# Loads on SyncE's queue, stores on ScalarE's: a change of issuing engines in a softmax with relative position bias

## The chip, the core and the metric

The kernel runs on one core of one Trainium2 chip. The metric is the device time of one execution in microseconds (us). VectorE, ScalarE and GpSimd compute here; SyncE only issues transfers; sixteen DMA engines move the bytes. TensorE does nothing.

## The reference

```python
B, H, S = 2, 8, 2112                       # logits: (B, H, S, S), float32
rel = clip(pos[:, None] - pos[None, :], -16, 16) + 16
x = logits + rel_bias[:, rel][None]        # rel_bias: (H, 33)
e = exp(x - x.max(-1, keepdims=True))
out = e / e.sum(-1, keepdims=True)         # float32
```

It reads 285.5 MB and writes 285.5 MB, and does little with each element.

## The kernel before

Each of the 128 partitions owns 264 rows. A chunk is six of them (6.49 MB over all partitions), so there are 44 chunks, and four buffers, `L0` to `L3`, go round. For a chunk, VectorE adds the bias (two adds of three rows), ScalarE takes the exps of the six rows with their sums, VectorE inverts the sums and scales; then the chunk is stored from the buffer it was loaded into. The maximum is not subtracted. A strip `F` of biases is built once at the start from the small table.

What the change touches is who issues the transfers:

```python
def store(eng, u, start, parts=1):
    take(eng, scaled, 1)                   # VectorE has scaled the chunk
    k = R // parts
    for r in range(0, R, k):
        eng.dma_start(out=rows(out, start + r, k * S), in_=L[u][:, r*S:(r+k)*S]).then_inc(stored[u], 16)

def reload(eng, u, start):
    take(eng, stored[u], 16)               # the buffer's last store has landed
    load(eng, u, start)

def sync_part(eng):
    row_load(eng, 0, first)                # rows 0, 2, 4 of chunk 0
    eng.wait_ge(loaded[BUFS - 2], 16)      # "the gate": the third load has landed
    passes(eng, 0, lambda u, start, loads: store(eng, u, start), N - BUFS)
    # ... (cut: the last four stores, and the waits for them)

def gpsimd_part(eng):
    row_load(eng, 1, loaded[0])            # rows 1, 3, 5 of chunk 0
    # ... (cut: two iotas for the strip)
    for n in range(1, BUFS):
        if n == BUFS - 1:
            take(eng, made, 1)             # buffer 3 was scratch for the strip
        load(eng, n, n * R)
    passes(eng, BUFS, lambda u, start, loads: reload(eng, u, start))
    eng.drain()

def scalar_part(eng):
    table_load(eng, range(B))
    # ... (cut: one small exp, which loads the activation table)
    passes(eng, 0, lambda u, start, loads: exps(eng, u))
```

## Time and profile before

| kernel before | |
|---|---|
| time, median of 3 runs | 1325.94 us (1325.87 to 1328.24) |
| bytes moved | 570.99 MB |
| VectorE, ScalarE, GpSimd busy | 71%, 40%, 3% |
| DMA queues' share of the engines | 50.4% + 49.3% |

First the list of DMA issues: what is moved, the issuing engine, how many, the size of each, and the median time in us from issue to landing.

```profile
L<-in_logits_dram POOLq DMA_DIRECT2D x43, 6336.0 KB, 39.1
out_dram<-L SPq DMA_DIRECT2D x42, 6336.0 KB, 55.3
```

A transfer of 6.49 MB would take 15 us with all engines to itself. It takes 39 or 55, because it queues behind others: in the steady state a transfer is nearly always waiting before the engines are free. Then the start, from the timeline (start us, length us, instruction, and in brackets the idle time before it and what ended that):

```profile
17.23 0.26 DVE L179 TENSOR_SCALAR L<-L,rbP 128x71 f32<-128x71 f32 x1 [12.51 <-DVEq L88]
...
24.88 13.43 DVE L118 TENSOR_TENSOR L<-L,F 128x6336 f32<-128x6336 f32 x2 [0.81 <-DVEq L88]
```

VectorE waits until 17.23 us for the bias table, finishes the strip and begins the first chunk's add at 24.88.

### The profile page before, as it was taken

The page shows a single profiled execution, that of the slowest core. Times are in us where ns is not written, and L with a number is a line of the kernel's source. Part 1 is how long each engine was busy: PE and PEld are TensorE (multiplying, and loading weights), DVE is VectorE, ACT ScalarE, POOL GpSimd, SP SyncE. Part 2 cuts the span into 40 slices and gives each one's busy share as a digit, 9 for nine tenths or more (in the row PEclk, how much of TensorE's full clock was granted, in tenths as well). Part 3 has the DMA queues.
Part 4 walks back from the last instruction along what each step waited for, and adds up shares of the span by engine and source line. Part 5 has one row for each costly group of instructions (what it writes and reads, how often), then busy time and mean ns, then how long its engine had stood idle before and what let it go on. Part 6 is the DMA issues. An engine that isn't in the chain of part 4 may idle for free. (4 is left out here: it accounts for less than half of the span.)

```text
span 1325.7 us, 2004 instructions
## 1 busy us (share of the span) xinstructions
DVE 941.8 (71%) x451; ACT 524.9 (40%) x530; POOL 35.1 (3%) x50
## 2 busy tenths in 40 slices
DVE  4989776677777767667777767667777767666891
ACT  0645533333444433333344443333344443333360
POOL 0000000000000000000000000000000000000000
DMA  9999999999999999999999999999999999999998
GB/s 392 434 432 430 439 433 433 433 437 431 428 439 439 431 427 439 437 431 430 439 434 427 437 439 430 428 439 437 433 428 437 437 430 433 437 433 428 432 444 349
DMA packets 13762, 570.99 MB, mean 431 GB/s; under 512 B 1600, under 2 KB 1600, under 8 KB 1600
## 3 DMA queue, kind: packets, MB, share of 16 engines
q1 hardware_dynamic: 7024, 288.72, 50.4%
q0 software_dynamic: 6592, 282.23, 49.3%
q10 hardware_dynamic: 144, 0.02, 0.0%
q14 instruction: 2, 0.02, 0.0%
HBM read 285.49 MB, written 285.47 MB: 431 GB/s over the span
## 5 line engine op out<-in xcount | busy, mean ns | idle before, releaser
L125 ACT ACTIVATE L<-L 128x2112 f32<-128x2112 f32 x264 | 515.2, 1952 | 767.9 <-ACTq L88 767.9
L118 DVE TENSOR_TENSOR L<-L,F 128x6336 f32<-128x6336 f32 x88 | 590.8, 6755 | 231.2 <-DMA L<-in_logits_dram 230.4
L139 DVE TENSOR_SCALAR L<-L,tot 128x2112 f32<-128x2112 f32 x264 | 332.7, 1317 | 13.2 <-DVEq L88 0.8
L135 DVE RECIPROCAL tot<-tot 128x3 f32<-128x3 f32 x88 | 15.2, 173 | 96.9 <-DVEq L88 96.9
L91 POOL DMA_DIRECT2D L<-in_logits_dram x43 | 33.8, 786 | 1208.2 <-POOLq L88 1208.2
L125 ACT ACTIVATION_READ_ACCUMULATOR L<-L 128x1 f32 x264 | 49.2, 186 | 0.0
L179 DVE TENSOR_SCALAR L<-L,rbP 128x71 f32<-128x71 f32 x1 | 0.3, 259 | 12.5 <-DVEq L88 12.5
L187 DVE TENSOR_TENSOR F<-L,rbP 128x2343 f32<-128x2343 f32 x1 | 2.6, 2601 | 0.1
L188 DVE TENSOR_TENSOR F<-F,L 128x2343 f32<-128x2343 f32 x1 | 2.6, 2600 | 0.1
L252 ACT ACT_TABLE_LOAD x1 | 1.3, 1283 | 2.9 <-issue 2.9
L174 DVE TENSOR_SCALAR L<-L 128x71 int32<-128x71 int32 x1 | 0.2, 197 | 3.1 <-DVEq L88 3.1
L177 DVE TENSOR_SCALAR L<-L 128x71 f32<-128x71 f32 x3 | 0.6, 198 | 0.4
L208 POOL DMA_DIRECT2D L<-in_logits_dram x1 | 0.9, 880 | 1.1 <-PEq L291 1.1
L182 DVE SCALAR_TENSOR_TENSOR L<-L,rbP 128x71 f32<-128x71 f32 x1 | 0.3, 294 | 0.2 <-DVEq L88 0.2
L175 DVE TENSOR_TENSOR L<-L 128x71 f32<-128x71 int32 x1 | 0.2, 236 | 0.1
L180 DVE COPY F<-rbP 128x16 f32<-128x16 f32 x1 | 0.2, 175 | 0.1
L186 DVE COPY F<-rbP 128x16 f32<-128x16 f32 x1 | 0.2, 176 | 0.1
L234 POOL IOTA L<- 128x71 int32 x1 | 0.2, 207 | 0.1
L237 POOL IOTA L<- 128x71 int32 x1 | 0.2, 208 | 0.0
L252 ACT ACTIVATE one<-const-float32-0.0 128x1 f32<-128x1 f32 x1 | 0.2, 203 | 0.0
L280 POOL MEMSET const-float32-0.0<- 128x1 f32 x1 | 0.1, 98 | 0.4 <-issue 0.4
L280 POOL MEMSET const-bfloat16-1.0<- 128x1 bf16 x1 | 0.1, 101 | 0.0
(2 smaller groups left out, 0.2 us busy)
## 6 DMA issues: line engine op xcount, KB each, us to landing
L<-in_logits_dram POOLq DMA_DIRECT2D x43, 6336.0 KB, 39.1
out_dram<-L SPq DMA_DIRECT2D x42, 6336.0 KB, 55.3
out_dram<-L SPq DMA_DIRECT2D x4, 3168.0 KB, 46.4
L<-in_logits_dram SPq DMA_DIRECT2D x1, 3168.0 KB, 15.7
L<-in_logits_dram POOLq DMA_DIRECT2D x1, 3168.0 KB, 18.3
rbP<-in_rel_bias_dram ACTq DMA_DIRECT2D x2, 8.2 KB
```

What stands on the lines that cost most here:

```text
L91: eng.dma_start(out=L[u][:], in_=rows(logits, start)).then_inc(loaded[u], 16)
L118: eng.tensor_tensor(out=x3, in0=x3, in1=F3, op=ALU.add).then_inc(added, 1)
L125: e = eng.activation(out=x, in_=x, func=EXP, accum_out=tot[u][:, i : i + 1])
L135: eng.reciprocal(out=t, in_=t).then_inc(inverted, 1)
L139: e = eng.tensor_scalar_mul(out=x, in0=x, scalar1=tot[u][:, i : i + 1])
L177: step(eng.tensor_scalar(out=m, in0=qm, scalar1=0.0, scalar2=None, op0=op))
L179: step(eng.tensor_scalar(out=rest, in0=lt, scalar1=low, scalar2=None, op0=ALU.mult))
L182: eng.scalar_tensor_tensor(out=rest, in0=gt, scalar=high, in1=rest, op0=ALU.mult, op1=ALU.add)
L187: step(eng.tensor_tensor(out=blocks, in0=wide(eq), in1=rev, op=ALU.mult))
L188: step(eng.tensor_tensor(out=blocks, in0=blocks, in1=wide(rest), op=ALU.add))
L208: eng.dma_start(out=bass.AP(tensor=x.tensor, offset=x.offset + r0 * S, ap=[[list(x.ap[0])[0], P], [2 * S, R // 2], [1, S]],), in_=bass.AP( ...
L252: eng.activation(out=one, in_=nc.const_aps.tensor(0.0, [P, 1], FP32), func=EXP)
```

## The change

The intent is to have loads and stores on the two hardware queues, one each, and to leave GpSimd's queue, whose descriptors are made in software, unused. SyncE issues all loads, the first chunk as two transfers of alternate rows. ScalarE issues each store after the exps of the chunk, once VectorE has scaled it.

```diff
     def sync_part(eng):
         row_load(eng, 0, first)
-        eng.wait_ge(loaded[BUFS - 2], 16)
-        passes(eng, 0, lambda u, start, loads: store(eng, u, start), N - BUFS)
-        ... (cut: the last four stores)
-    def gpsimd_part(eng):
         row_load(eng, 1, loaded[0])
-        ... (cut: the iotas, which stay with GpSimd)
         for n in range(1, BUFS):
             if n == BUFS - 1:
                 take(eng, made, 1)
             load(eng, n, n * R)
         passes(eng, BUFS, lambda u, start, loads: reload(eng, u, start))
-        eng.drain()
+        ... (cut: the waits for the last four stores)
     def scalar_part(eng):
-        passes(eng, 0, lambda u, start, loads: exps(eng, u))
+        def whole(u, start, loads):
+            exps(eng, u)
+            if u == 0:
+                eng.wait_ge(loaded[BUFS - 2], 16)
+            store(eng, u, start)
+        passes(eng, 0, whole, N - BUFS)
+        for n in range(BUFS):
+            exps(eng, n)
+            store(eng, n, (N - BUFS + n) * R, 2 if n < 2 else 1)
```

More of the change, by code (lines that the diff above doesn't have):

```diff
@@ L222, in sync_part @@
         row_load(eng, 0, first)
-        eng.wait_ge(loaded[BUFS - 2], 16)
-        passes(eng, 0, lambda u, start, loads: store(eng, u, start), N - BUFS)
-        for n in range(BUFS):
-            store(eng, n, (N - BUFS + n) * R, 2 if n < 2 else 1)
+        row_load(eng, 1, loaded[0])
+        for n in range(1, BUFS):
+            if n == BUFS - 1:
+                take(eng, made, 1)
+            load(eng, n, n * R)
+        passes(eng, BUFS, lambda u, start, loads: reload(eng, u, start))
         for n in range(BUFS):
@@ L232, in gpsimd_part @@
     def gpsimd_part(eng):
-        row_load(eng, 1, loaded[0])
         eng.iota(qi, pattern=[[0, NB]], base=0, channel_multiplier=M).then_inc(
@@ L239, in gpsimd_part @@
         )
-        for n in range(1, BUFS):
-            if n == BUFS - 1:
-                take(eng, made, 1)
-            load(eng, n, n * R)
-        passes(eng, BUFS, lambda u, start, loads: reload(eng, u, start))
-        eng.drain()
     def scalar_part(eng):
```

## The prediction

> **What bounds the kernel now.** I read the page of the profile first: busy shares, the forty slices, then the queues.
>
> ```profile
> DVE 941.8 (71%) x451; ACT 524.9 (40%) x530; POOL 35.1 (3%) x50
> ...
> DMA  9999999999999999999999999999999999999998
> GB/s 392 434 432 430 439 433 433 433 437 431 428 439 439 431 427 439 437 431 430 439 434 427 437 439 430 428 439 437 433 428 437 437 430 433 437 433 428 432 444 349
> ...
> q1 hardware_dynamic: 7024, 288.72, 50.4%
> q0 software_dynamic: 6592, 282.23, 49.3%
> q10 hardware_dynamic: 144, 0.02, 0.0%
> ```
>
> No compute engine is near full, while the DMA row is 9 in every slice but the last, and the two large queues together fill 99.7% of the sixteen engines' time. 570.99 MB have to move; the rate lies about 434 GB/s in 38 slices, 392 in the first, 349 in the last. Next I cut the run into stretches, to see the rate without the ends and with one queue alone (columns: stretch, its length, busy us of VectorE, ScalarE and GpSimd, the clock, DMA share, GB/s).
>
> ```profile
> 20.00:50.00 30.00, 26.54 (x13) 11.90 (x12) 0.53 (x1) 1.00 1.00 433
> 100.00:1240.00 1140.00, 818.17 (x385) 459.36 (x463) 31.12 (x38) 1.00 1.00 434
> 1275.00:1320.00 45.00, 22.53 (x12) 11.90 (x12) 0.00 (x0) 1.00 1.00 432
> ```
>
> The middle line is the steady state, loads from GpSimd's queue and stores from SyncE's side by side: 434 GB/s. The first is loads alone (the DMA view of that stretch lists only the software queue), the third stores alone from SyncE's hardware queue. All three give the same rate with the engines full, so the sixteen DMA engines are the bound, whatever the mix of queues. 570.99 MB / 434 GB/s = 1315.6 us; the other 10 us are ends: in the first 3.3 us the engines are little used (the DMA view from 0 to 33 us starts with digits 0 0 7 5), 8,448-byte packets run at some 410 GB/s from 5 to 15 us, and after 1320 us only 17 GB/s flow, the last landing.
>
> How far is compute from being the bound? The list of waits and one chunk of the timeline (start, length, engine, instruction):
>
> ```profile
> POOL L L91 <- POOLq L88: 1208.2, 41, 56.5
> ACT L L125 <- ACTq L88: 767.9, 88, 27.3
> DVE L L118 <- DMA L<-in_logits_dram: 230.4, 38, 6.4
> ...
> 505.65 13.43 DVE L118 TENSOR_TENSOR L<-L,F 128x6336 f32<-128x6336 f32 x2 [6.23 <-DMA L<-in_logits_dram]
> ...
> 525.62 3.78 DVE L139 TENSOR_SCALAR L<-L,tot 128x2112 f32<-128x2112 f32 x3 [0.15 <-DVEq L88]
> ```
>
> From the first add to the last scaling of a chunk are 525.62 + 3.78 - 505.65 = 23.75 us; a chunk comes every 30 us (two loads and stores of 6.49 MB at 434 GB/s: 29.9). VectorE waits 6.2 us per chunk for the load: that is the slack of the compute chain. The load's median from issue to landing is 39.1 us, the store's 55.3; over 30 us that is 1.3 loads and 1.8 stores in flight on average, so both queues hold work nearly always.
>
> **What the Trainium skill says.** (1) "DMA: Bandwidth & Descriptors", section "Issuing engines are not separate DMA queues": transfers from ScalarE, SyncE and GpSimd run on the same sixteen engines and interleave; spreading the issue saves only sequencer time. The three stretches agree: 433, 434, 432. (2) Same page, "Where 436 GB/s comes from": sixteen ports give 435.2 GB/s. The 434 agrees, and it leaves at most 0.3% (1315.6 - 570.99/435.2 = 3.6 us) for any better queue. The same section says the HBM side, about 358, binds such transfers; this trace, one core alone, does not show that. (3) "SBUF — State Buffer", section "SBUF: two separate sides": while VectorE runs an instruction in a two-port mode, GpSimd can't write its descriptors; a hardware queue isn't affected. The trace agrees: a load issue lasts 0.53 us usually, yet the one at 825.41 took 1.35 and ended at 826.76, just after the first of the scalings that began at 825.32 (1.315 us each, so 826.64). (4) First page, "Latency and other measured facts": first byte after some 0.6 us on a hardware queue, some 1 us on GpSimd's.
>
> **The change, part by part.**
> - Loads: 43 issues leave GpSimd (786 ns mean, 33.8 us busy in all) for SyncE, where an issue took 332 ns. On average a load starts 786 - 332 = 0.45 us sooner, 1 us where the scaling blocked it. Nothing of it is on the path that sets the end: when a load is issued the one before has 39.1 - 30 = 9 us to go, and stores are queued. Value: 0.
> - Stores: 46 issues go to ScalarE, behind each chunk's exps. Cost on ScalarE: 332 ns as on SyncE, up to 0.91 us as its own two table loads took (median), so 15 to 42 us over the run on an engine busy 525 of 1326 us. ScalarE also stands still until the chunk is scaled. But VectorE runs in order: the next chunk's first add (6.75 us) begins only after that scaling, and the exps need that add. So at least 6.75 - 0.91 = 5.8 us are left over for the issue in every chunk. Value: 0.
> - First chunk: both halves stand in SyncE's queue one behind the other. The bytes are the same and sixteen engines work from the first half on; it lands by about 2 + 3.24 MB / 410 GB/s = 10 us instead of 16.8, the second by about 18 instead of 19.9. The bias table's packets (18 on each engine that carries them: 144 over 8, the 8 my reading of the access pattern) now alternate with one large queue, not two: estimate 9 to 12 us instead of 17.2. The strip of biases takes 17.23 to 24.08, 6.9 us, so the first add should start at 18 to 20 us instead of 24.88. This is not turned into time: the first store still waits for the third load, at about 50 us, and the DMA engines are full from 3.3 us. I give 0 to -1 us.
> - Gate on the first store now holds ScalarE: the exps of chunk 1 could begin about 49 us and begin at about 50.5; before they began at 55.4. No loss.
> - End: same four last stores, same halves; loads end some 45 us before the end. GpSimd's drain goes, beside nothing. Value: 0.
>
> Sum: 1325.9 + 0 + 0 - 0.5 + 0 is about 1325; with noise of the runs (1325.87 to 1328.24) I keep 1325.
>
> **Rivals.**
> (a) The software queue had a hidden cost, and two hardware queues come nearer to the ceiling: at most 3.6 us for the rate and 1 us at the start: 1321. For it: blocked issues. Against: engines at share 1.00 with it.
> (b) ScalarE becomes part of the chain: if the issue cost or blocked for longer than the 5.8 us left and the 6.2 us slack, say 15 us per chunk, a chunk would take 23.75 + 15 - 5.8 = 33 us, or 1450 in all. For it: an issue could be held up while descriptors are made or a ring is full. Against: SyncE issued the same stores in 332 ns (482 at most), also with four of them queued at the end.
> (c) Two hardware queues disturb each other, one share starving the other or reads and writes mixing worse. If stores were favoured, loads would land later; once they take more than 6 us longer the slack is gone only if in-flight work runs out, since four buffers hold 120 us: 39.1 + 55.3 + 23.75 = 118. A loss of 1% in rate makes 1338. Against: nothing in this trace shows two large hardware queues together, so I can't exclude it; this is my main doubt.
> (d) Earlier compute at the start shortens the whole: would be up to 6 us if compute were the bound; the full DMA row speaks against it.
>
> **Range and chances.** 1325 us, eight times in ten between 1320 (all of rival a) and 1332 (half a percent for rival c). Faster by over 2% would need 1299, below the 1311.9 us which the bytes take at 435.2: 0.01. Slower by over 2%, above 1352, needs (b) or a strong (c): 0.04. Within 2%: 0.95.
>
> **What would show it.** Right: DMA share 1.00 and 433 to 435 GB/s from 100 to 1240 us; the queues' shares 50/50, now both hardware; load plus store landing still about 94 us; VectorE still waiting about 6 us per chunk for loads; GpSimd's 34 busy us gone; store issues on ScalarE under 1 us; the first add at 18 to 20 us, the first store still near 50. Wrong: a steady rate under 430, slices below 9 in the middle, ScalarE's issue over 2 us, or VectorE's waits moved from loads to sums.

## The result, and the profile after

The changed kernel took 1327.14 us (median of 4 runs, 1326.46 to 1328.04), the kernel before 1327.09 us in 4 runs (1325.87 to 1329.13). The ratio is 0.9999, with a 95% interval from 0.9982 to 1.0017: the same. Ratios here are the mean time of one kernel's fast runs over the mean of the other's fast runs of the same rounds, so not quite the ratio of the medians that are quoted.

The page of the changed kernel, the same lines as in the prediction:

```profile
DVE 941.5 (71%) x451; ACT 524.9 (40%) x530; POOL 0.5 (0%) x6
...
DMA  9999999999999999999999999999999999999998
GB/s 395 433 430 432 436 438 424 436 441 436 424 438 439 427 435 438 436 424 438 441 425 433 439 436 424 438 439 435 425 439 438 425 435 439 438 424 436 433 434 363
...
q1 hardware_dynamic: 6992, 285.48, 49.9%
q10 hardware_dynamic: 6768, 285.49, 49.8%
```

GpSimd's 35 us are gone, both large queues are hardware now, and the DMA rows look as before. The stretches (loads alone, steady state, stores alone) say it in numbers; the last column is GB/s:

```profile
20.00:50.00 30.00, 26.84 (x11) 11.90 (x12) 0.00 (x0) 1.00 1.00 433
...
100.00:1240.00 1140.00, 815.75 (x385) 459.99 (x465) 0.00 (x0) 1.00 1.00 434
...
1275.00:1320.00 45.00, 20.96 (x10) 11.90 (x12) 0.00 (x0) 1.00 1.00 433
```

They were 433, 434 and 432. The waits, one chunk of the timeline, and the DMA issues:

```profile
DVE L L117 <- DMA L<-in_logits_dram: 234.3, 39, 6.3
```

```profile
503.89 13.43 DVE L117 TENSOR_TENSOR L<-L,F 128x6336 f32<-128x6336 f32 x2 [6.23 <-DMA L<-in_logits_dram]
...
523.86 3.78 DVE L138 TENSOR_SCALAR L<-L,tot 128x2112 f32<-128x2112 f32 x3
...
527.88 0.34 ACTq L96 DMA_DIRECT2D out_dram<-L  x1
533.86 13.43 DVE L117 TENSOR_TENSOR L<-L,F 128x6336 f32<-128x6336 f32 x2 [6.22 <-DMA L<-in_logits_dram]
540.73 1.96 ACT L124 ACTIVATE L<-L 128x2112 f32<-128x2112 f32 x1 [17.34 <-ACTq L87]
```

```profile
L<-in_logits_dram SPq DMA_DIRECT2D x43, 6336.0 KB, 37.2
out_dram<-L ACTq DMA_DIRECT2D x42, 6336.0 KB, 58.0
```

The add of one chunk begins 29.97 us after that of the one before, and VectorE still waits 6.2 us for the load in each. ScalarE issues the store at 527.88, in 0.34 us, and its next exp begins only at 540.73, when the next add is done: 12.5 us lie between. Loads land 1.9 us sooner, stores 2.7 us later; the sum, 95.2 us, is nearly the 94.4 of before.

The start did move:

```profile
13.01 0.26 DVE L178 TENSOR_SCALAR L<-L,rbP 128x71 f32<-128x71 f32 x1 [9.87 <-DVEq L87]
...
20.66 13.43 DVE L117 TENSOR_TENSOR L<-L,F 128x6336 f32<-128x6336 f32 x2 [0.81 <-DMA L<-in_logits_dram]
...
44.32 13.42 DVE L117 TENSOR_TENSOR L<-L,F 128x6336 f32<-128x6336 f32 x2
50.44 0.38 ACTq L96 DMA_DIRECT2D out_dram<-L  x1
51.20 1.96 ACT L124 ACTIVATE L<-L 128x2112 f32<-128x2112 f32 x1 [11.04 <-ACTq L87]
```

The table came 4.2 us sooner, the first add too; now it waits for the second half of its rows, not for the strip. None of it is seen in the time. It is the loads' side of the change that brings it: in the half-change below, where only the stores moved, the table was again in use at 16.95 us and the first add began at 24.60.

### The profile page after: what moved, and what is told of

Same layout as the page of the kernel before. It is cut to its first block, busy times and chain, and to the rows that moved or that the text cites. A ratio compares the mean times of both kernels' runs of the same rounds, so it can differ in the third digit from the quotient of the medians.

```text
span 1325.0 us, 1980 instructions
## 1 busy us (share of the span) xinstructions
DVE 941.5 (71%) x451; ACT 524.9 (40%) x530; POOL 0.5 (0%) x6
## 2 busy tenths in 40 slices
DMA packets 13763, 570.99 MB, mean 431 GB/s; under 512 B 1601, under 2 KB 1601, under 8 KB 1601
## 3 DMA queue, kind: packets, MB, share of 16 engines
q1 hardware_dynamic: 6992, 285.48, 49.9%
q10 hardware_dynamic: 6768, 285.49, 49.8%
## 5 line engine op out<-in xcount | busy, mean ns | idle before, releaser
L134 DVE RECIPROCAL tot<-tot 128x3 f32<-128x3 f32 x88 | 15.2, 173 | 96.7 <-DVEq L87 96.7
## 6 DMA issues: line engine op xcount, KB each, us to landing
L<-in_logits_dram SPq DMA_DIRECT2D x43, 6336.0 KB, 37.2
```

Of the source, the lines that this page charges most:

```text
L134: eng.reciprocal(out=t, in_=t).then_inc(inverted, 1)
```

## The experiments

The theory: the sixteen DMA engines set the time, at 434 GB/s whatever queue feeds them; the changes on the issuing side lie in slack. The rivals: two effects of opposite sign cancel (ScalarE's waiting costs, leaving the software queue gains), or the slack is not where I read it. Eleven kernels ran, each beside the kernel before.

### Half of the change: only the stores move

Loads stay on GpSimd, stores go to ScalarE as in the changed kernel.

```diff
 def sync_part(eng):             # against the changed kernel
     row_load(eng, 0, first)
-    row_load(eng, 1, loaded[0]); the loads; the reloads
     ... the waits for the last four stores
 def gpsimd_part(eng):
+    row_load(eng, 1, loaded[0]); the iotas; the loads; the reloads; drain
```

In the first version the final waits stood on GpSimd, ahead of its drain.

> Half of the change: the stores move to ScalarE behind the exps, the loads stay on GpSimd. Theory (the sixteen DMA engines are the bound and no issuer matters): 1327 us, within 0.3% of both kernels, DMA share 1.00 and 433 to 435 GB/s in the steady state. Rival (two effects of opposite sign cancel: ScalarE's waiting costs, leaving the software queue gains): this half alone is slower by more than 0.5%, over 1333 us.

It took 1330.86 us, ratio 1.0024 (1.0008 to 1.0041): slower by a quarter of a per cent, which neither side had foreseen. The trace shows that it was no matter of rate. The last packet ended at 1324.3 us, as in the kernel before (1324.0), but the program ended 5.1 us after it instead of 1.7; in the last 7 us next to nothing moved, and SyncE waited 27.7 us until GpSimd's end:

```profile
1322.00:1329.00 7.00, 0.00 (x0) 0.00 (x0) 0.00 (x0) 1.00 0.02 7
```

```profile
SPq L73 <- POOLq L73: 27.7, 1, 27.7
```

My own placing of the last waits was the suspect. So I gave the last four stores semaphores of their own, on which SyncE waits, as in both kernels.

```diff
-    for n in range(BUFS): take(eng, stored[n], ...)    # on GpSimd, then drain
+    for n in range(BUFS): take(eng, done[n], ...)      # on SyncE
```

> The first half-change again, with the final waits on SyncE as in both kernels (the first version had put them on GpSimd, ahead of its drain; its transfers ended by 1322 us like the others', and its end came 6 us later). Theory: the 3.5 us of the first version were that ending alone, so now 1325 to 1329 us, ratio to the kernel before within 0.2% of 1. Rival (ScalarE issuing the stores beside the software queue really costs 0.25%, and SyncE's loads give it back): again about 1331 us, ratio 1.002 or more.

1326.12 us, ratio 0.9995 (0.9978 to 1.0013), 434 GB/s. Half of the change alone costs nothing, so nothing had to be given back by the other half: the cancelling of two effects falls, for anything larger than the 0.2% of the interval. The lesson on the side is that the engine whose instructions come last can lengthen a kernel by some 4 us, though it does no work. Whether GpSimd's waits or its drain behind them took the time was not tested.

### Everything in one queue

```diff
 def sync_part(eng):             # the loads as in the changed kernel, then
+    eng.wait_ge(loaded[BUFS - 2], 16)
+    store(eng, 0, 0)
+    for each later chunk n: store(chunk n - 3); reload(chunk n)
 def scalar_part(eng):
-    exps, then store
+    exps
```

> All loads and all stores in SyncE's one hardware queue, in the order store of chunk n-3, then refill of chunk n. Theory: still 1325 to 1332 us, since one queue alone already carried 433 (loads) and 432 GB/s (stores) in the kernel before; steady rate 433 to 435. Rival (it is two queues side by side that fill the engines; one queue, with reads and writes one after the other, loses at each turn): steady rate under 428 and over 1345 us.

1330.82 us, ratio 1.0029 (1.0012 to 1.0046). The steady rate was 433 GB/s, so one queue that turns between reads and writes fills the engines nearly as well as two. Counted from the packets of the traces it was 433.4 against 433.9 in the changed kernel, which is about half of the loss: at 1240 us this kernel was 0.6 MB (1.4 us) behind. The rest came at the end, in this stretch (the changed kernel, then this one):

```profile
1300.00:1310.00 10.00, 0.00 (x0) 0.00 (x0) 0.00 (x0) 1.00 0.94 406
```

```profile
1300.00:1310.00 10.00, 3.96 (x5) 2.07 (x4) 0.00 (x0) 1.00 0.88 380
```

VectorE was still scaling the last chunk after 1300 us, until 1306; in the changed kernel it had ended at 1298.5. In a single queue loads land at 44.8 us instead of 37.2, so the last chunk comes later (its first add begins at 1282.6 us), and the engines run short of stores while it is computed; that this is the whole cause is my reading, not tested. The mix of queues hardly matters here for the rate, but the order can for the last chunk.

### Both kernels with few bytes to store

If the DMA engines hide a cost, it must come out where they are not the bound. Both kernels were cut to store one row of six. Their outputs are wrong, which doesn't matter for the times.

```diff
-        k = R // parts
-        for r in range(0, R, k):
+        k = 1
+        for r in range(0, parts):
```

> The kernel before, but only one row of six of each chunk is stored (the result is wrong on purpose), so about 335 MB move instead of 571 and compute becomes the bound. Theory: the first add starts at about 24.9 us, 44 chunks of 23.66 us follow (1041 us), some 5 us for the last small store: 1071 us. If the software queue has a cost that the full DMA engines hid, VectorE's scalings get longer or it waits for loads, and the chunk is over 24.0 us (over 1085).

> The same cut in the changed kernel. Theory: first add at 20.7 us, 44 chunks of 23.66 us, 5 us at the end: 1067 us, 4 us (0.4%) under the cut kernel before, from the earlier start alone. If ScalarE's waiting and store issue have a cost that the full DMA engines hid, the chunk is longer by up to the issue's 0.4 us: up to 1085 us and slower than the cut kernel before.

The kernel before took 1072.54 us so, the changed one 1069.01, 3.5 us less, near the 1071 and 1067 expected. The adds show why. The kernel before, then the changed one, both from their timelines:

```profile
24.75 13.43 DVE L118 TENSOR_TENSOR L<-L,F 128x6336 f32<-128x6336 f32 x2 [0.81 <-DVEq L88]
48.41 13.42 DVE L118 TENSOR_TENSOR L<-L,F 128x6336 f32<-128x6336 f32 x2
```

```profile
21.33 13.43 DVE L117 TENSOR_TENSOR L<-L,F 128x6336 f32<-128x6336 f32 x2 [0.81 <-DMA L<-in_logits_dram]
45.00 13.42 DVE L117 TENSOR_TENSOR L<-L,F 128x6336 f32<-128x6336 f32 x2
```

A chunk takes 23.66 and 23.67 us, and VectorE waits for no load after the first. The first add begins 3.4 us sooner, and that is the whole difference. So neither the software queue nor ScalarE's double duty has a cost per chunk that is seen in this loop, bound by DMA or, with one row of six stored, by compute; what the change is worth is its start, and only where the bytes aren't the bound.

### How much slack ScalarE has

Between the end of a chunk's scaling and the issue of its store, ScalarE was made to take four, then eight exps into a scratch place, for chunks 0 to 39.

```diff
             exps(eng, u)
+            take(eng, scaled, 1)
+            for _ in range(8):             # 4 in the first run
+                eng.activation(out=junk[:], in_=F[:, :2048], func=EXP).then_inc(held, 1)
+                take(eng, held, 1)
+            eng.sem_inc(scaled, 1)
             ...
             store(eng, u, start)
```

> The changed kernel with four exps into a scratch place (some 2 us each, 8 us in all) on ScalarE between the end of a chunk's scaling and the issue of its store, chunks 0 to 39. Theory: 13 us stand free on ScalarE there (6.75 us of the next add and 6.2 us of VectorE's wait for the load), so the time stays at 1325 to 1332 us, with the store issued 8 us later and VectorE's wait for loads unchanged or shorter. Rival (ScalarE's hold in front of the issue is on the path already): 40 times 8 us would make 1647 us; half of it 1487.

> The same with eight exps, 16 us, which is more than the 13 us that are free. Theory: ScalarE and VectorE now form the chain, a chunk takes 16 us of hold, 0.5 us of issue and 16.9 us from the first exp to the scaling, 33.4 us, so 44.4 + 39 x 33.4 + 16.4 + 16.9 + 3 x 23.7 + some 20 us for the last store: 1455 to 1475 us, DMA share under 0.95. If the time stays under 1350, the chain as I read it is wrong.

With four (7.9 us) the time was 1329.24 us, ratio 1.0013 (0.9996 to 1.0029), at 433 GB/s: of 40 times 7.9 us nearly all was hidden. The mean is 1.7 us longer, and the interval allows anything from nothing to 3.9 us. With eight it was 1459.2 us. The timeline of that run:

```profile
506.68 13.42 DVE L120 TENSOR_TENSOR L<-L,F 128x6336 f32<-128x6336 f32 x2
506.89 15.88 ACT L254 ACTIVATE junk<-F 128x2048 f32<-128x2048 f32 x8 [4.37 <-ACTq L90]
523.15 0.34 ACTq L99 DMA_DIRECT2D out_dram<-L  x1
539.56 13.42 DVE L120 TENSOR_TENSOR L<-L,F 128x6336 f32<-128x6336 f32 x2
```

```profile
100.00:1240.00 1140.00, 737.78 (x350) 926.11 (x692) 0.00 (x0) 1.00 0.96 389
```

A chunk now takes 32.9 us, the next 33.3, where 33.4 had been worked out, and VectorE no longer waits for loads but for sums. The break lies between 8 and 16 us, as the 13 us of slack say. The DMA share reads 0.96 here (under 0.95 had been expected), at 389 GB/s, which is 90% of 434: a load's packet took 2.08 us on average between 100 and 1000 us, in the changed kernel 1.87. So the share alone does not tell a full engine; read it beside GB/s.

### A dearer issue

Each store was issued as six, one for each row.

```diff
-        k = R // parts
+        k = 1
```

> The changed kernel with every store issued as six, one per row, so ScalarE spends six times 0.34 us, 2.0 us, on the issue of a chunk instead of 0.34, and packets of stores are 8448 bytes instead of 50688. Theory: the issue's 1.7 us more are hidden (1325 to 1332 us); if the time grows, the steady rate of the engines must have fallen with the smaller packets, not the waits of ScalarE. Rival (ScalarE's issue is on the path): 44 x 1.7 = 75 us more, 1402 us.

1358.0 us, ratio 1.0234 (1.0213 to 1.0255). The rate fell to 423 GB/s at full share. But the issues were far from 0.34 us. The changed kernel, then this one (shortest, median, longest in ns):

```profile
L96 ACTq DMA_DIRECT2D out_dram<-L x46: 338/339/478, 50.4 to 1298.6; - x46
```

```profile
L96 ACTq DMA_DIRECT2D out_dram<-L x264: 337/343/13171, 50.5 to 1341.9; - x132
```

```profile
519.04 11.43 ACTq L96 DMA_DIRECT2D out_dram<-L  x6
530.60 1.96 ACT L124 ACTIVATE L<-L 128x2112 f32<-128x2112 f32 x1 [16.06 <-ACTq L87]
```

One issue could be held 13 us, the six of a chunk took 11.4 in this one, and the next exps began only after. This is the second rival of the prediction, the issue that is held up; it had been argued away from stores with few packets. The waits moved as well: VectorE no longer waited for loads (0.8 us in all), but for sums, where the changed kernel has 96.7 us:

```profile
DVE tot L134 <- DVEq L87: 369.0, 85, 9.2
```

Two causes for the 31 us were now open: smaller packets, and the hold. Two more runs were to part them.

```diff
+        for r in range(2):          # rows r, r+2, r+4: packets of one row, two issues
+            eng.dma_start(out=[[T*S, P], [2*S, 3], [1, S]], in_=..., ).then_inc(stored[u], 16)
```

> Six issues per store cost 31 us in the changed kernel, with the engines still full but at 423 GB/s, and with ScalarE held 11 to 16 us in its issues. This run keeps the packets of 8448 bytes and takes the hold away: two issues per store, each of three alternate rows. If the packet size is the cause: 423 GB/s and 1350 to 1360 us again, with issues of 0.34 us. If ScalarE's hold is the cause: 434 GB/s and 1325 to 1332 us.

> The kernel before (loads on GpSimd, stores on SyncE) with every store issued as six. SyncE may be held in its issues as ScalarE was, but no compute stands behind it. If the packet size is the cause of the 31 us: the same 1355 to 1360 us. If ScalarE's hold is the cause: 1325 to 1332 us; if both, between.

Two issues per store of one-row packets: 1363.91 us, ratio 1.0269 (1.0221 to 1.0318), 424 GB/s. As a separation this failed: the hold was still there, with issues of 5.7 us in the median and 13.9 at most. So it is not the number of issues alone that matters but what they put in the queue: 50 packets for each engine and store here (800 over 16), 54 with six issues (864 over 16), 9 in the changed kernel (144 over 16). The kernel before with six issues is the cleaner test. SyncE was held too, up to 16.8 us, but no compute stands behind it:

```profile
L97 SPq DMA_DIRECT2D out_dram<-L x264: 332/2064/16797, 50.6 to 1325.7; - x132
```

It took 1351.02 us, ratio 1.0167 (1.0121 to 1.0212, which leaves open whether it is slower by 2%), at 425 GB/s. That lies between the two times expected, which was to mean both causes. So most of the loss, 23 to 24 of 31 us, comes without any hold of ScalarE, and the rate accounts for it: 570.99 MB at 425 GB/s take 1343.5 us, 28 more than at 434. That the packets' size lowers the rate is the likely reading, since all three kernels with one-row packets run at 423 to 425, and the first chunk's loads, alone and in packets of that size, ran at 409 to 411 GB/s in the kernel before (5 to 15 us); other sizes were not tried. Whether the 7 to 13 us that ScalarE's versions take beyond that come from the hold stays open. With two issues VectorE still waited for loads (263.7 us in all; 250.9 in the kernel before with six), so ScalarE's hold was not the wait that ended last there, and yet this kernel was the slowest.

### Without the gate

The wait for the third load ahead of chunk 0's store was taken out of the changed kernel.

```diff
-            if u == 0:
-                eng.wait_ge(loaded[BUFS - 2], 16)
```

> The changed kernel without the wait for the third load ahead of chunk 0's store, so the store goes out at about 44.5 us instead of 50.4. Theory: the engines are full in any case, so 1325 to 1329 us. Rival (the start is worth its 6 us): about 1321 us.

The first store went out at 44.50 us instead of 50.44, and the time was 1331.64 us, ratio 1.0015 (0.9973 to 1.0058); 1325 to 1329 had been expected. No gain of 6 us is to be seen, so the rival falls; whether there is a small loss instead is inconclusive, since one run of the kernel before was at 1337.25 us in these rounds. In the profiled run (a span of 1334.9 us) little moved in the last 13 us, with one or two engines busy on average. Why that was is open.

## Why the prediction was right

**The bound.** Right: 1327.14 us lies two microseconds from the 1325 predicted. The half microsecond that the sum gives to the start is too small to be told from noise. Its main step, that the sixteen engines set the time whatever the mix of queues, was shown by 434 GB/s before and after, by 433 in one queue, by the half-change at 0.9995, and by the cut pair, where fewer bytes made the time shorter by 19%. (A slip without effect: 570.99 MB at 435.2 GB/s take 1312.0 us, not 1311.9.)

**Loads.** Right that the quicker issue is worth nothing here: GpSimd's busy time went from 35.1 to 0.5 us, loads land 1.9 us sooner, and VectorE's wait stayed at 6.2 us a chunk. In the cut pair, where loads don't queue, they land in 17.5 us instead of 17.9, so the gain per load is about 0.4 us; it is real and hidden. Of the prediction's points from the skill, two can be read here. None of the 43 load issues on SyncE was held by a scaling: they took 0.33 us, 0.48 at most, on GpSimd up to 1.61. And from the start of an issue to the first packet of its load the cut pair shows 1.23 us (median) for GpSimd and 0.96 for SyncE, so a smaller difference than the 1 and 0.6 us quoted.

**Stores.** Right, and on the careful side. The issue took 0.34 us, at the low end of the range given. At least 5.8 us had been counted as left over; with the wait for the load it is about 12.5, and the two holds put the break between 8 and 16 us. The size given to the rival, a chunk of 33 us with a hold of 15, came out as 33.0 on average with 15.9, for which the same sum gives 33.9.

**First chunk.** Right in direction and in its worth, mis-sized: the table was to be in use by 9 to 12 us and was at 13.0, the second half of the first chunk to land by 18 us and landed at 20.3, so the first add began at 20.7 instead of 18 to 20. The terms that failed: for the table, its packets came on eight engines, as counted, but the first began only at 5.5 us and the last landed at 12.9. For the rows, a mean rate was taken, but a transfer ends with its slowest engine: in sum 3.24 MB had been moved by about 10.5 us, while the sixteen engines ended the first half between 10.8 and 12.3, and the second between 18.5 and 20.2. Why the table's packets began so late stays open.

**Gate and end.** Right that nothing is lost, but the gate was not the wait that ended last: it was to hold the exps of chunk 1 until about 50.5 us. The store was issued by 50.82, and the exps began at 51.20, held by the add (44.32 + 6.75 = 51.07), which came from the later first add.

**Rivals.** (a), a gain of up to 4 us, is not seen: the rate was already there. (c), two hardware queues that disturb each other, was the main doubt and fell: 434 GB/s, 49.9% and 49.8%. (d), the earlier start, is worth 3.5 us in the cut pair, where compute is the bound, and nothing that is seen here. (b), the held issue, does not occur in this change, but the argument against it held only for stores of 9 packets per engine; with 50 or 54 it occurs.

## What to carry to other kernels

Compare bytes over the measured rate with the time first: where they nearly agree and one queue alone already reaches that rate, as here, moving transfers between issuing engines has little left to gain but at the start and the end. Before giving stores to an engine that computes, find its free stretch from the timeline (here 12.5 us a chunk), and keep the packets large, because both the rate and the length of an issue got worse with one-row packets. Where a change moves nothing, cut the load on the bound in both kernels and compare again: that shows whether a cost or a gain was merely hidden.

## What the Trainium skill lacked or had wrong

- "DMA: Bandwidth & Descriptors", section "Issuing engines are not separate DMA queues", calls the sequencer's time to initiate a transfer usually small beside the transfer. With 50 or 54 packets per engine and store, single issues lasted up to 13.9 us on ScalarE and 16.8 us on SyncE; with 9 they lasted 0.34 us. When an issue is held is not told there; "Perfetto Trace Analysis", section "DMA Instruction — HWDGE (DVE, Sync)", says that descriptors can be more than their buffer holds, but gives no number.
- The same page asks for at least 1 MiB per DMA ("Rules for kernel authors") and puts the least size for the full rate at 512 bytes ("Specifications"). Here transfers of 1 to 3 MB in packets of 8448 bytes ran at 423 to 425 GB/s beside loads of large packets, against 434 with packets of 50688.
- The same page, section "Where 436 GB/s comes from", lets the HBM side (about 358) bind such transfers, without the condition that its section on bandwidth has: that both cores of the pair stream. One core alone moved 434 GB/s here, reads and writes together.
- "Perfetto Trace Analysis", section "Identifying the Most-Contended Engine", calls the occupancy of the DMA engines misleading, but does not say by how much. Here the busy share read 0.96 at 389 GB/s, which is 90% of 434, and 0.79 at 324 (the cut pair), which is 75%.
